# Where the expert scatter and the slot products stand in TensorE's row: tying them behind the next pair's up product

## The chip, the cores and the metric

The kernel runs on one core of a Trainium2 chip. The metric is the device time of one execution in microseconds (us): the median over the runs shown. Beside it stands one execution taken by the hardware profiler, whose trace gives the start and length of the instructions on TensorE (PE), its weight loads (PEld), VectorE (DVE), ScalarE (ACT), GpSimd (POOL) and the DMA queue of SyncE (SP).

## The reference

Two layers of a transformer trunk over 256 tokens of width 1024. Each layer is a token mixer (forgetting attention in layer 0, latent attention under a chunk mask in layer 1, "mixer B" below) and then a mixture of experts. 16 experts of width 512 stand in 4 groups; a router takes the best group of each token and two experts in it. Cut to the experts, for one layer:

```
h    = modulate(rmsnorm(x), shift, scale)
idx  = the two experts of each token, in its best group
g, u = h @ w_gate[e], h @ w_up[e]            # 1024 -> 512, for each expert e
y_e  = (silu(g) * u * routing_weight) @ w_down[e]   # 512 -> 1024
x    = x + gate * sum over a token's two experts of y_e
```

Everything is float32.

## The kernel before, in words

The experts are worked on in pairs, i = 0 to 7 in each layer, 64 token slots for each expert, so a pair fills 128 rows. `P[g]` are one-hot matrices of group g (two pairs) that say which token sits in which slot. The accumulators of the new x stay in four PSUM banks (0 to 3: two token halves by two column halves) for the whole expert stage. One pair goes like this:

- `wide("g", i, 4)` and `wide("u", i, 5)` (line 899): the gate product into bank 4 and the up product into bank 5, 16 matmuls each, two instructions in the trace for one matmul (float32). The weights come in pieces of at most 1 MB. After a product `done` gives the pieces' buffers back.
- silu on ScalarE (line 985), then `act`, the product of silu, up product and routing weight, on VectorE (line 996).
- four transposes of act into bank 4 (line 1003), copied to `aT` half by ScalarE, half by VectorE (lines 1006, 1007).
- the down product (line 1018) in two column halves, banks 6 and 7. Behind it VectorE multiplies by the layer's gate (`yb`, line 1031) and splits the result in two parts for a pass in a reduced float format (`yh`, lines 1033, 1034).
- `scatter(i)` (line 911): eight matmuls that add the pair's result into banks 0 to 3 by the transposed one-hot matrix `PT[i]`. It is written in pair i + 1, behind that pair's act. For the last pair it is written out behind each part of the down product (line 1044), followed by copies of x (line 1049, layer 0) or products with the final gain (`xg`, line 739, layer 1).
- `slots(i + 1, 5)` (line 883): two products that turn the one-hot matrix of the next pair, and VectorE's evictions of them (`PT`, and the routing weights `cs` that the next pair's act needs).
- after odd pairs, `fetch` (line 869): four times eight matmuls that gather the next group's tokens.

Before the up product of pair 4 (`OV`) stands a branch to an overflow path, which is not taken in the profiled execution (line 917).

All weights come over one DMA queue, on SyncE, in a fixed order through ten buffers of 1 MB (line 250) and some smaller tiles that are free in a stage (`Pieces`, line 262). A piece is issued when its buffer has been given back, so the queue waits for the product that read the buffer before.

The order of the instructions on each engine is set by a scheduler that works from the code's data dependences and its own estimate of times. It may put a scatter matmul anywhere behind its inputs: between down products, between gate products, or singly. `tc.issue_after(ins)` adds one rule: what is written inside stands behind the instruction `ins` on that engine. PSUM banks 4 and 5 serve in turn for gate, up, transposes, gathers and slot products.

Of the kernel before, what the change touches and what calls it, by code (L numbers as in the profile page):

```python
# [38 lines left out]
E = 16  # L39
# [4 lines left out]
OV = 4  # L44
# [29 lines left out]
def trunk_kernel(ctx, tc, A, out):  # L74
# [10 lines left out]
    def bank(i):  # L85
        return psp.tile([128, 512], F32, name=f"b{i}", tag=f"b{i}")
# [11 lines left out]
    def wide_rows(nm, l, i):  # L98
        return ((0, 4), (4, 2), (6, 2)) if l and nm == "u" and i == E // 2 - 1 else ((0, 4), (4, 4))
# [104 lines left out]
    u = A["kv_w_up"].rearrange("(p k) (a n) -> p k a n", k=2, a=2)  # L204
# [66 lines left out]
    def get(name):  # L271
        assert name in live, name
        return live[name]
# [11 lines left out]
    def done(name):  # L285
        assert stream[state["used"]][0] == name, (stream[state["used"]][0], name)
        drop()
        mods()
# [10 lines left out]
    def behind(i):  # L299
        return tc.issue_after(state["after"][i]) if state["after"][i] else ExitStack()  # L300
# [172 lines left out]
    def fin_bc(name, tag):  # L473
        rows = mod_rows(name)
        g_ = big.tile([128, D], F32, name=tag)
        ps = bank(MB)
        for h in range(2):
            if h:
                ps = bank(MB)
            for q in range(2):  # L480
                PE.matmul(ps[:, 256 * q:256 * q + 256], pick[:, 2 * h + q:2 * h + q + 1].to_broadcast([128, 128]), rows,
                          start=True, stop=True)
            SC.activation(g_[:, 512 * h:512 * h + 512], ps, AF.Copy)
        M[name] = g_
# [262 lines left out]
    def moe(l, G, sh, acc):  # L747
# [83 lines left out]
        def onehot(g):  # L831
            P[g] = wk.tile([128, T, 4, CAP], F32R, name="P", tag="zef", bufs=1)
            for t in range(T):
                at = V.tensor_tensor(P[g][:, t], iotas[:, None, :].to_broadcast([128, 4, CAP]),  # L834
                                     pos[:, t, 4 * g:4 * g + 4, None].to_broadcast([128, 4, CAP]), op=ALU.is_equal)
            return at.ins
# [43 lines left out]
        def slots(i, b):  # L880
            ps = bank(b).rearrange("p (t n) -> p t n", t=T)[:, :, 0:2 * E + 128]
            for t in range(T):
                PE.matmul(ps[:, t], P[i // 2][:, t, 2 * (i % 2):2 * (i % 2) + 2].rearrange("p e s -> p (e s)"), idc[:, t],
                          start=True, stop=True)
            PT[i] = wk.tile([128, T, 128], F32R, name="PT")
            V.tensor_copy(PT[i], ps[:, :, 2 * E:])
            for e in range(2):
                part = ps[64 * e:64 * e + 64, :, 0:2 * E].rearrange("p t (j e) -> p t j e", j=2)
                V.tensor_reduce(cs[64 * e:64 * e + 64, i:i + 1], part[:, :, :, 2 * i + e], axis=AX.XY, op=ALU.add)

        def wide(nm, i, b):
            ps = bank(b)
            for c, (k0, nk) in enumerate(wide_rows(nm, l, i)):
                ws = [get((nm, l, i, c, e)) for e in range(2)]
                for kk in range(nk):
                    k = k0 + kk
                    for e in range(2):
                        o = 128 * (i % 2) + 64 * e
                        last = PE.matmul(ps[64 * e:64 * e + 64, :], XG[i // 2, k // 4][:, k % 4, o:o + 64], ws[e][:, kk, :],  # L899
                                         start=k == 0, stop=k == 7).ins  # L900
                if i == 0 and nm == "g":
                    after[5] = last
                for e in range(2):
                    done((nm, l, i, c, e))
            return ps

        def scatter(i):
            for half in range(2):
                for t in range(T):
                    for j in range(2):  # L910
                        PE.matmul(acc[t, half], PT[i][:, t, :], yh[:, j, 512 * half:512 * half + 512],  # L911
                                  start=False, stop=False)
# [63 lines left out]
        for i in range(E // 2):  # L976
            pg = wide("g", i, 4)
            if i == OV:
                scatter(i - 1)
                overflow()  # L980
            if l and i == 0 and G2IN:
                with behind(5):
                    fin_bc("g2_1", "g2")
            sg = wk.tile([128, F], F32, name="sg", tag="t2", bufs=3)
            SC.activation(sg, pg, AF.Silu)  # L985
            if i == 0:
                slots(0, SL0)
                if l == 0:
                    with tc.issue_after(late):
                        rotary()  # L990
            turn_over = i % 2 and i < E // 2 - 1
            if turn_over:
                onehot(i // 2 + 1)
            pu = wide("u", i, 5)
            a = wk.tile([128, F], F32, name="act", tag="t2", bufs=3)
            V.scalar_tensor_tensor(a, sg, cs[:, i:i + 1], pu, op0=ALU.mult, op1=ALU.mult)  # L996
            if i and i != OV:
                scatter(i - 1)
            if l and i == 2:
                final_gain()  # L1000
            pa = bank(4)
            for k in range(4):
                PE.transpose(pa[:, 128 * k:128 * k + 128], a[:, k::4], ident)  # L1003
            aT = wk.tile([128, 4, 128], F32, name="aT", tag="t2", bufs=3)
            pav = pa.rearrange("p (a b) -> p a b", a=4)
            SC.activation(aT[:, 0:2], pav[:, 0:2], AF.Copy)  # L1006
            V.tensor_copy(aT[:, 2:4], pav[:, 2:4])
            if turn_over:
                for c in range(2):
                    fetch(i // 2 + 1, c, (5, 4)[c])  # L1010
            cols = down_cols(l, i)
            for p, (c0, n) in enumerate(cols):
                py = bank(6 + p % 2)
                cs_ = slice(c0, c0 + n)
                ws = [get(("d", l, i, p, e)) for e in range(2)]
                for k in range(4):
                    for e in range(2):
                        at = PE.matmul(py[64 * e:64 * e + 64, 0:n], aT[:, k, 64 * e:64 * e + 64], ws[e][:, k, :],  # L1018
                                       start=k == 0, stop=k == 3).ins
                if i == OV - 1 and p == 1:  # L1020
                    with tc.issue_after(at):
                        tc.mark_branch_hint_location(f"over{l}", "LikelyTaken", [mybir.EngineType.PE])
                for e in range(2):
                    done(("d", l, i, p, e))
                if p == 0 and turn_over:
                    for c in range(2, 4):
                        fetch(i // 2 + 1, c, (5, 4)[c % 2])
                if p == 0 and i < E // 2 - 1:
                    slots(i + 1, 5)
                yb = big.tile([128, 512], F32, name="yb", bufs=2)  # L1030
                V.tensor_tensor(yb[:, 0:n], py[:, 0:n], M[f"g2_{l}"][:, cs_], op=ALU.mult)  # L1031
                if len(cols) == 2 or p == 0:
                    SC.activation(yh[:, 0, cs_], yb, AF.Copy)  # L1033
                    V.tensor_tensor(yh[:, 1, cs_], yb, yh[:, 0, cs_].bitcast(F32), op=ALU.subtract)
                    parts_ = [(PT[i], yh[:, j, cs_]) for j in range(2)]
                else:
                    parts_ = [(PT[i].bitcast(F32), yb[:, 0:n])]
                if i == E // 2 - 1:
                    half, o = c0 // 512, c0 % 512
                    if l == 0 and p == 0:  # L1040
                        x.new()
                    for t in range(T):
                        for j, (pt, y_) in enumerate(parts_):
                            PE.matmul(acc[t, half][:, o:o + n], pt[:, t, :], y_, start=False,
                                      stop=o + n == 512 and j == len(parts_) - 1)
                        if o + n == 512:
                            ch = slice(512 * half, 512 * half + 512)
                            if l == 0:
                                V.tensor_copy(x[:, t, ch], acc[t, half])
                            squares(t, half, None, acc[t, half])  # L1050
                    if l and o + n == 512:
                        gains(half, acc)
# [69 lines left out]

    accs = attention(0, maskA, 1.0, proj_a, "wo0", "g1_0")
    moe(0, M["sc2_0"], M["sh2_0"], accs)


# [263 lines left out]
```

## Time and profile before

| | us |
|---|---|
| median of 3 runs | 857.45 (856.47 to 857.65) |
| profiled execution | 856.38 |
| its span in the trace | 854.3 |
| PE busy | 767.0 (90%) |
| DVE busy | 376.0 (44%) |
| ACT busy | 266.6 (31%) |
| POOL busy | 166.2 (19%) |

The mean granted TensorE clock was 0.97 of full speed. 294.30 MB were read from device memory, 346 GB/s over the span. The span begins with the first instruction of the trace and ends with the last; the profiled execution is 2.1 us longer, which lies around it. Busy shares are means over four stages: mixer A to about 207 us, experts of layer 0 to about 447, mixer B with the router to about 622, experts of layer 1 to the end.

### The profile page before, as it was taken

How to read it: one execution, taken by the hardware profiler on the slowest of the kernel's cores; microseconds unless marked ns; L12 is line 12 of the kernel's file. 1: busy time of each engine (PE TensorE's matmuls, PEld its weight loads, DVE VectorE, ACT ScalarE, POOL GpSimd, SP SyncE). 2: the span in 40 equal slices, each digit the busy share in tenths (PEclk: the TensorE clock that was granted, in tenths of full speed). 3: DMA queues.
4: the chain of work that ended last, by engine and by line, in shares of the span. 5: the costliest groups of instructions: out<-in, count | busy, mean ns of one | idle time of the engine just before them, and what ended most of it. 6: DMA issues, size and time to landing. Idle time of an engine off the chain costs nothing.

```text
span 854.3 us, 11932 instructions
## 1 busy us (share of the span) xinstructions
PE 767.0 (90%) x4522; PEld 441.9 (52%) x4522; DVE 376.0 (44%) x831; ACT 266.6 (31%) x578; POOL 166.2 (19%) x151
## 2 busy tenths in 40 slices
PE   4678999998999999899978798999799999999994
PEld 2477888765344343243327666777533534434332
DVE  2389599977112211221238949665712321122112
ACT  2346456534101011010127555765511110111002
POOL 1273567320000000000007755321100000000000
PEclk9699999999999999999998999999799999999998
DMA  9997897899999999999997769768789999999992
GB/s 347 383 376 272 275 347 261 315 380 392 414 397 394 417 402 403 418 407 403 414 397 270 231 226 362 293 222 273 269 292 402 402 374 413 367 393 398 402 392 82
DMA packets 102855, 296.32 MB, mean 347 GB/s; under 512 B 6992, under 2 KB 26624, under 8 KB 90496
## 3 DMA queue, kind: packets, MB, share of 16 engines
q1 hardware_dynamic: 101968, 293.79, 90.8%
q10 hardware_dynamic: 288, 1.05, 0.3%
q8 instruction: 39, 0.64, 0.3%
q0 software_dynamic: 528, 0.59, 0.2%
q14 instruction: 32, 0.26, 0.1%
HBM read 294.30 MB, written 1.05 MB: 346 GB/s over the span
## 4 chain that ended last, share of the span: by engine, by line
issue 28%; PE 23%; DVE 5%; DMA 2%; ACT 1%; POOLq 0%; POOL 0%; SPq 0%; another core or an unknown queue 0%; DVEq 0%; ACTq 0%
PE b L899 6%; PE b L1018 4%; PE b L522 2%; PE b L523 2%; PE b L524 2%; DVE macc L329 1%; DMA fg<-in_final_norm_g_dram 1%; PE b L911 1%; PE b L631 1%; DMA w<-in_w_mod_dram 1%; DVE wl L518 1%; DMA w<-in_exp_w_gate_dram 1%; PE b L321 1%; PE b L557 1%; PE b L593 1%
## 5 line engine op out<-in xcount | busy, mean ns | idle before, releaser
L899 PE MATMUL b<-w,XG 128*64 128x512 f32 x1024 | 239.0, 595 | 0.6 <-PEq L917 0.6
L518 POOL TENSOR_TENSOR wl<-w,wh 128x512 fp32r<-128x512 f32 (+3 forms) x90 | 132.4, 1487 | 354.0 <-ACT wh L517 350.5
L899 PEld LDWEIGHTS b<-w,XG 128*64 128x64 f32 x1024 | 78.2, 137 | 140.8 <-issue 135.3
L1018 PE MATMUL b<-w,aT 128*64 128x512 f32 (+1 forms) x528 | 125.8, 585 | 3.7 <-ACT aT L1006 3.7
L996 DVE SCALAR_TENSOR_TENSOR act<-sg,rcs,b 128x512 f32<-128x512 f32 x16 | 12.0, 747 | 211.3 <-PE b L899 211.3
L517 ACT ACTIVATE wh<-w 128x512 fp32r<-128x512 f32 (+3 forms) x136 | 76.6, 587 | 63.3 <-PE b L524 22.7
L1018 PEld LDWEIGHTS b<-w,aT 128*64 128x64 f32 x528 | 38.2, 136 | 66.0 <-issue 56.2
L329 DVE SCALAR_TENSOR_TENSOR macc<-w,cact,macc 128x1024 f32<-128x1024 f32 x42 | 63.6, 1513 | 1.2 <-DMA w<-in_w_mod_dram 0.7
L1033 ACT ACTIVATE yh<-yb 128x512 fp32r<-128x512 f32 x31 | 19.6, 631 | 113.2 <-DVE yb L1031 113.2
L518 DVE TENSOR_TENSOR wl<-w,wh 128x512 fp32r<-128x512 f32 (+2 forms) x46 | 44.3, 973 | 19.8 <-ACT wh L517 19.7
L1031 DVE TENSOR_TENSOR yb<-b,g 128x512 f32<-128x512 f32 (+1 forms) x33 | 22.2, 674 | 64.1 <-PE b L1018 64.1
L985 ACT ACTIVATE sg<-b 128x512 f32<-128x512 f32 x16 | 9.6, 598 | 119.9 <-PE b L899 119.9
L539 POOL TENSOR_TENSOR rs<-rs,mhalf 128x1 f32<-128x1 f32 (+1 forms) x9 | 5.4, 602 | 206.6 <-DVE rs L538 206.6
L321 PE MATMUL b<-w,cact 128*32 128x256 f32 x512 | 39.9, 418 | 6.0 <-DMA w<-in_w_mod_dram 5.7
L524 PE MATMUL b<-h,wl 128*128 128x256 f32 (+1 forms) x136 | 40.5, 299 | 4.7 <-DVE wl L518 4.3
L522 PE MATMUL b<-h,wh 128*128 128x256 f32 (+1 forms) x136 | 40.3, 300 | 3.5 <-ACT h L579 3.5
L1006 ACT ACTIVATE aT<-b 128x256 f32<-128x256 f32 x16 | 6.1, 384 | 117.1 <-PE b L1003 117.1
L869 PEld LDWEIGHTS b<-P,xs 128*128 128x128 f32 x256 | 34.4, 203 | 15.2 <-DVE XG L875 6.5
L869 PE MATMUL b<-P,xs 128*128 128x256 f32 x256 | 39.3, 304 | 1.6 <-DVE P L834 1.6
L523 PE MATMUL b<-h,wh 128*128 128x256 f32 (+1 forms) x136 | 39.5, 292 | 0.0
L911 PE MATMUL b<-yh,PT 128*128 128x512 f32 x112 | 34.4, 422 | 2.1 <-ACT yh L1033 2.1
L523 PE MATMUL b<-wl,h 128*128 128x256 f32 (+1 forms) x96 | 30.0, 316 | 2.9 <-POOL wl L518 2.4
(296 smaller groups left out, 1208.8 us busy)
## 6 DMA issues: line engine op xcount, KB each, us to landing
w<-in_exp_w_down_dram SPq DMA_DIRECT2D x50, 1024.0 KB, 12.5
w<-in_w_mod_dram SPq DMA_DIRECT2D x48, 1024.0 KB, 8.9
w<-in_exp_w_gate_dram SPq DMA_DIRECT2D x48, 1024.0 KB, 12.8
w<-in_exp_w_up_dram SPq DMA_DIRECT2D x48, 1024.0 KB, 13.0
w<-in_a_w_in_dram SPq DMA_DIRECT2D x12, 1024.0 KB, 12.4
w<-in_exp_w_gate_dram SPq DMA_DIRECT2D x42, 256.0 KB, 7.2
w<-in_exp_w_up_dram SPq DMA_DIRECT2D x40, 256.0 KB, 5.9
w<-in_kv_w_mod_dram SPq DMA_DIRECT2D x8, 1024.0 KB, 7.0
```

The lines of the kernel that those rows point to most:

```text
L321: PE.matmul(acc[32 * q:32 * q + 32, :], cact[:, k:k + 1].to_broadcast([128, 32]), w[:, kk, 256 * q:256 * q + 256], start=k == 0, stop=k == 7)
L329: V.scalar_tensor_tensor(acc, w[:, kk, :], cact[:, k:k + 1], acc, op0=ALU.mult, op1=ALU.add)
L517: SC.activation(hi, src, AF.Copy)
L518: lo_eng.tensor_tensor(lo, src, hi.bitcast(F32), op=ALU.subtract)
L522: PE.matmul(ps, l[0], r_[0], start=start, stop=False)
L523: PE.matmul(ps, l[0], r_[1], start=False, stop=False)
L524: PE.matmul(ps, l[1], r_[0], start=False, stop=stop)
L869: at = PE.matmul(ps[:, 256 * kk:256 * kk + 256], xs[n % 2, n // 2][:, 128 * k:128 * k + 128], P[g][:, n // 2].rearrange("p e s -> p (e s)" ...
L899: last = PE.matmul(ps[64 * e:64 * e + 64, :], XG[i // 2, k // 4][:, k % 4, o:o + 64], ws[e][:, kk, :], start=k == 0, stop=k == 7).ins
L911: PE.matmul(acc[t, half], PT[i][:, t, :], yh[:, j, 512 * half:512 * half + 512], start=False, stop=False)
L1018: at = PE.matmul(py[64 * e:64 * e + 64, 0:n], aT[:, k, 64 * e:64 * e + 64], ws[e][:, k, :], start=k == 0, stop=k == 3).ins
L1031: V.tensor_tensor(yb[:, 0:n], py[:, 0:n], M[f"g2_{l}"][:, cs_], op=ALU.mult)
```

## The change

In each pair, what stands in the code behind act now gets a rule: it is to stand behind the last matmul of that pair's up product on TensorE. In pairs 1 to 3 and 5 to 7 that is the scatter of the pair before. In pairs 0 and 4 there is none (the scatter of pair 3 stays ahead of the overflow branch, without a rule), and the slot products for the next pair are put there, in bank 7 in place of bank 5 and no longer behind the first half of the down product.

```
                 if i == 0 and nm == "g":
                     after[5] = last
+                ends[nm] = last
...
+        ends = {}
...
             a = wk.tile([128, F], F32, name="act", tag="t2", bufs=3)
             V.scalar_tensor_tensor(a, sg, cs[:, i:i + 1], pu, op0=ALU.mult, op1=ALU.mult)
-            if i and i != OV:
-                scatter(i - 1)
+            with tc.issue_after(ends["u"]):
+                if i in (0, OV):
+                    slots(i + 1, 7)
+                else:
+                    scatter(i - 1)
...
-                if p == 0 and i < E // 2 - 1:
+                if p == 0 and i < E // 2 - 1 and i not in (0, OV):
                     slots(i + 1, 5)
```

The changed kernel has six lines more, so its scatter is line 914, its transposes 1009, its down products 1024 and the last pair's scatter 1050. The first place is TensorE's row from pair 4 of layer 0 to the transposes of pair 5. Before (b_5958 is the second half of pair 4's down product, b_5975 and b_6005 are gate and up of pair 5, b_1736 to b_1739 the accumulators):

```order
L911 MATMUL b_1736<-yh,PT 128x512
L911 MATMUL b_1738<-yh,PT 128x512
L1018 MATMUL b_5958<-w,aT 64x512 x7
L899 MATMUL b_5975<-w,XG 64x512
L911 MATMUL b_1737<-yh,PT 128x512
L911 MATMUL b_1739<-yh,PT 128x512
L899 MATMUL b_5975<-w,XG 64x512 x15
L899 MATMUL b_6005<-w,XG 64x512 x16
L1003 MATMUL b_6040<-idc,act 128x128 x4
```

The same stretch of the changed kernel:

```order
L1024 MATMUL b_5958<-w,aT 64x512 x8
L899 MATMUL b_5975<-w,XG 64x512 x16
L899 MATMUL b_6005<-w,XG 64x512 x16
L914 MATMUL b_1736<-yh,PT 128x512 x2
L914 MATMUL b_1738<-yh,PT 128x512 x2
L914 MATMUL b_1737<-yh,PT 128x512 x2
L914 MATMUL b_1739<-yh,PT 128x512 x2
L1009 MATMUL b_6040<-idc,act 128x128 x4
```

The scatter of pair 4 stood in three pieces in and behind its own down product and inside the gate product of pair 5; now it is one run between the up product and the transposes. In both layers the transposes of pairs 1 to 3 and 5 to 7 now have such a run ahead of them, and those of pairs 0 and 4 have the two slot products. Before, a run stood there in three places: pair 1 of layer 0, and pairs 1 and 3 of layer 1.

The second place is VectorE's row at the end of layer 0's experts, from the first half's yh (b_6316 and b_6346 are the two halves of pair 7's down product; the wl are weight splits for mixer B). Before:

```order
L1034 TENSOR_TENSOR yh<-yb,yh 128x512
L1049 COPY x<-b_1736 128x512
L1049 COPY x<-b_1738 128x512
L518 TENSOR_TENSOR wl<-w,wh 128x288 x2
L1031 TENSOR_TENSOR yb<-b_6346,g_2389 128x512
```

The same stretch of the changed kernel:

```order
L1040 TENSOR_TENSOR yh<-yb,yh 128x512
L518 TENSOR_TENSOR wl<-w,wh 128x288
L1055 COPY x<-b_1736 128x512
L518 TENSOR_TENSOR wl<-w,wh 128x288
L1055 COPY x<-b_1738 128x512
L518 TENSOR_TENSOR wl<-w,wh 128x288
L1037 TENSOR_TENSOR yb<-b_6346,g_2389 128x512
```

One weight split has moved ahead of the yb of the second half. On TensorE the last two of the four scatter matmuls that these copies wait for now stand two matmuls before the end of the down product; before, all four stood behind its first matmul of that half.

The third place is TensorE's row at the end of layer 1 (b_12263 is the first half of pair 7's down product, b_12288 and b_12301 are two quarters, b_7767 to b_7770 the accumulators). Before:

```order
L1003 MATMUL b_12255<-idc,act 128x128 x4
L1018 MATMUL b_12263<-w,aT 64x512 x8
L1018 MATMUL b_12288<-w,aT 64x256 x8
L1018 MATMUL b_12301<-w,aT 64x256 x8
L1044 MATMUL b_7767<-yh,PT 128x512
L1044 MATMUL b_7769<-yh,PT 128x512
```

The same stretch of the changed kernel:

```order
L914 MATMUL b_7770<-yh,PT 128x512 x2
L1009 MATMUL b_12255<-idc,act 128x128 x4
L1024 MATMUL b_12263<-w,aT 64x512 x8
L1024 MATMUL b_12288<-w,aT 64x256 x8
L1024 MATMUL b_12301<-w,aT 64x256
L1050 MATMUL b_7767<-yh,PT 128x512
L1050 MATMUL b_7769<-yh,PT 128x512
L1050 MATMUL b_7767<-yh,PT 128x512
L1050 MATMUL b_7769<-yh,PT 128x512
L1024 MATMUL b_12301<-w,aT 64x256 x7
```

The scatter of pair 6 now stands ahead of the transposes, and the first half's own scatter stands behind one matmul of the last quarter in place of all eight. At the start of layer 1's experts, five modulation matmuls stood ahead of the first gate product on TensorE; one does now, and the other four stand inside and behind that product. In mixer B, where no line has changed, the scheduler has put many instructions of all engines in another order.

## Rows read from the trace of the kernel before

**Rows 1.** The page: GB/s moved, in 40 equal slices of the span.

```profile
GB/s 347 383 376 272 275 347 261 315 380 392 414 397 394 417 402 403 418 407 403 414 397 270 231 226 362 293 222 273 269 292 402 402 374 413 367 393 398 402 392 82
```

**Rows 2.** Stretches: from:to, length, busy us (count) by engine, clock, DMA share, GB/s.

```profile
215.00:440.00 225.00, 213.03 (x999) 85.36 (x996) 43.11 (x87) 26.13 (x46) 0.55 (x1) 1.00 1.03 407
625.00:836.00 211.00, 204.21 (x950) 83.75 (x948) 42.20 (x87) 24.11 (x44) 0.61 (x1) 1.00 1.01 386
...
350.00:360.00 10.00, 7.93 (x32) 2.67 (x32) 2.50 (x4) 1.26 (x2) 0.00 (x0) 1.00 1.01 422
...
470.00:480.00 10.00, 7.46 (x44) 6.10 (x43) 9.91 (x17) 4.68 (x8) 9.21 (x9) 1.00 0.45 140
...
610.00:620.00 10.00, 6.71 (x44) 5.80 (x43) 5.36 (x27) 1.69 (x3) 0.00 (x0) 0.54 0.58 222
```

**Rows 3.** Waits of the DMA queue, whole span: us in total, times, longest.

```profile
SPq L250 <- PE b L899: 111.8, 49, 8.1
```

**Rows 4.** Waits of TensorE from 200 us on: us in total, times, longest.

```profile
PE b L1003 <- DVE act L996: 11.1, 12, 0.9
```

**Rows 5.** Timeline of TensorE, layer 0, pair 4: start, length, instruction, idle before.

```profile
344.72 0.75 PE L1003 MATMUL b<-idc,act 128*128 128x128 f32 x4 [0.92 <-DVE act L996]
...
357.62 1.46 PE L911 MATMUL b<-yh,PT 128*128 128x512 f32 x4 [1.44 <-ACT yh L1033]
...
373.87 0.75 PE L1003 MATMUL b<-idc,act 128*128 128x128 f32 x4 [0.91 <-DVE act L996]
```

**Rows 6.** Timeline of TensorE, layer 1, pair 2 to pair 3.

```profile
693.47 0.75 PE L1003 MATMUL b<-idc,act 128*128 128x128 f32 x4 [0.93 <-DVE act L996]
...
715.55 2.14 PE L911 MATMUL b<-yh,PT 128*128 128x512 f32 x8
717.53 0.63 PE L1003 MATMUL b<-idc,act 128*128 128x128 f32 x4
```

**Rows 7.** DMA queue, last up pieces of layer 0: issues, then time to landing.

```profile
L250 SPq DMA_DIRECT2D w<-in_exp_w_up_dram x2: 328/356/385, 411.7 to 412.2; - x2
...
DMA to landing us min/median/max: 12.7/13.7/14.8
```

**Rows 8.** Timeline of TensorE, end of layer 0: last up matmuls, transposes of pair 7.

```profile
428.25 4.03 PE L899 MATMUL b<-w,XG 128*64 128x512 f32 x16
...
433.19 0.75 PE L1003 MATMUL b<-idc,act 128*128 128x128 f32 x4 [0.91 <-DVE act L996]
```

**Rows 9.** Timeline of TensorE, end of layer 1.

```profile
829.30 2.31 PE L899 MATMUL b<-w,XG 128*64 128x512 f32 x8
...
832.51 0.75 PE L1003 MATMUL b<-idc,act 128*128 128x128 f32 x4 [0.91 <-DVE act L996]
...
843.68 2.06 PE L1044 MATMUL b<-yb,PT 128*128 128x256 f32 x8 [1.65 <-DVE yb L1031]
```

**Rows 10.** Timeline of VectorE, end of layer 0.

```profile
440.93 1.29 DVE L1049 COPY x<-b 128x512 f32<-128x512 f32 x2 [0.59 <-PE b L1044]
```

**Rows 11.** The page's groups: instruction, count, busy, mean ns, idle before.

```profile
L329 DVE SCALAR_TENSOR_TENSOR macc<-w,cact,macc 128x1024 f32<-128x1024 f32 x42 | 63.6, 1513 | 1.2 <-DMA w<-in_w_mod_dram 0.7
```

**Rows 12.** Timeline of the DMA queue, start of layer 1's experts.

```profile
620.22 5.99 SPq L250 DMA_DIRECT2D w<-in_exp_w_up_dram  x2
```

**Rows 13.** Timeline of TensorE, ahead of layer 1's first gate product.

```profile
621.23 1.05 PE L321 MATMUL b<-w,cact 128*32 128x256 f32 x10
```

**Rows 14.** DMA queue, last up pieces of layer 1: issues, then time to landing.

```profile
L250 SPq DMA_DIRECT2D w<-in_exp_w_up_dram x2: 328/356/383, 814.5 to 814.9; - x2
...
DMA to landing us min/median/max: 9.3/9.8/10.2
```

**Rows 15.** DMA queue, last down pieces of layer 1: issues, then time to landing.

```profile
L250 SPq DMA_DIRECT2D w<-in_exp_w_down_dram x2: 540/540/540, 827.4 to 828.2; - x2
...
DMA to landing us min/median/max: 7.6/7.9/8.1
```

**Rows 16.** Timeline of VectorE, end of layer 1.

```profile
842.60 0.69 DVE L739 TENSOR_TENSOR xg<-b,fg 128x512 f32<-128x512 f32 x1 [2.97 <-ACT junk L532]
```

## The prediction

> **What bounds the kernel now.** I read the page's slices first. Its row of bytes moved shows two long runs of slices with some 400 GB/s, the ninth to the 21st (171 to 448 us) and the 31st to the 39th (641 to 833) [rows 1]. Those are the two expert stages. The view by stretches says the same in numbers: 1.03 and 1.01 of the engines' time, 407 and 386 GB/s, with TensorE busy for 213 of 225 us and 204 of 211 us [rows 2]. So two things are nearly full at once, and which of them sets a stage's end has to be worked out. A pair of experts reads three matrices of 2 MiB for each of two experts, 12.58 MB; at 407 GB/s that is 30.9 us. The DMA queue's own waits say that it stands mostly behind products that still hold its buffers [rows 3]. The queue is therefore held back by TensorE in its issues, but the engines under it never run dry: earlier issues make a longer line and not more bytes in a microsecond.
>
> TensorE's own largest wait is the one that the change aims at: the transposes wait for act 12 times, 11.1 us in all, 0.9 us each [rows 4].
>
> **What each pair gains on TensorE.** In pair 4 of layer 0 the transposes start at 344.72, those of pair 5 at 373.87 [rows 5]: 29.15 us. Inside are the wait for act (0.91 at its end), a wait of 1.44 for yh because the second half of the scatter stands straight behind the down product, and lone products between scatter pieces. The form that the change gives to pairs exists before, whole, in one place, from pair 2's transposes in layer 1 to pair 3's: down, gate, up, the eight scatter products in one run, and then the transposes without a wait, 693.47 to 717.53 = 24.06 us; the run of eight costs 1.98 (715.55 to 717.53) [rows 6]. So pair 4 can save 29.15 - 24.06 = 5.1. Worked in the same way from the starts of the other transposes, layer 0 could save about 16 us (pairs 2 and 6: 2.4 each, pair 3: 2, pair 5: 3.5, the first wait 0.9) and layer 1, where less was scattered, about 9. In pairs 0 and 4 two slot products (0.43) cover part of the wait of 0.91; what is left, 0.5 twice a layer, is inside these numbers. No arithmetic is added, and no transfer.
>
> **What the weights let through in layer 0.** A pair in the new form takes 24.06 us, its weights 30.9. TensorE can only use the lead that the weights still have. The last pieces of layer 0's up product are issued at 411.7 to 412.2 and land at most 14.8 us later, so the last at 426.9 [rows 7]. The up product's last 16 matmul rows begin at 428.25, and the second expert's first is two rows in, at 428.68 [rows 8] (a row is 0.215: 16 of them take 4.03, eight take 2.31 [rows 9]). The lead is 1.77 us. That is all that the end of the up product can gain, of the 16. Behind it now stands the scatter: the transposes of pair 7 come at 433.19 [rows 8] - 1.77 - 0.91 (the wait for act, now covered) + 1.97 = 432.5, a gain of 0.7. Then the order of layer 0's end changes: VectorE now has two copies of x (1.29 for the two [rows 10]) and two weight splits between the last scatter product into their banks and the second half's yb, where before they ran while the down product was still at work. As the bank that x copies is finished two matmuls (four rows, 0.86) before the down product's end, I put the delay at 1.1, with 0 and 1.7 as bounds. Layer 0 as a whole: 0.7 - 1.1 = **0.4 lost**.
>
> **The mixer between.** The scheduler orders mixer B anew as well, on all engines; no line of the diff is in it. VectorE is busy for 9.91 of 10 us at 470 to 480, so one of the modulation steps of 1.51 us [rows 2, 11] that is put ahead of work that TensorE needs, or behind it, moves the end by about its length. I find moves in both directions and no reason for a sign: **0, bounds 2.5 either way**.
>
> **What the weights let through in layer 1.** The weight stream of this layer restarts behind releases of TensorE (between its first two issues, 5.99 us from 620.22 on [rows 12]), and the gate product now starts behind two of ten modulation rows (1.05 us from 621.23 [rows 13]). So the whole stream comes about **0.8 earlier** (bounds 0 and 0.9). The last up pieces are issued at 814.9 and land 10.2 later at the latest, at 825.1 [rows 14]; their use is two rows behind 829.30, at 829.73 [rows 9]. The lead is 4.6, and with the earlier stream the up product can end 5.4 earlier. TensorE offers 9, so the weights decide again. As in layer 0 the scatter (1.97) takes the place of the wait (0.91): the transposes come at 832.51 - 5.4 + 1.06 = 828.2. The down pieces do not hold this up: the last are issued at 828.2 and land within 8.1 [rows 15], at 836.3 and with the earlier stream at 835.5, and their use moves behind four scatter products, to about 836.5.
>
> At the end TensorE now issues the four scatter products of the first half after one matmul of the last quarter, not after all of them. Before, yb of a quarter stood on VectorE behind xg, which came 2.97 us after the work before it, when those scatter products had been read once [rows 16], and TensorE then idled 1.65 for a yb [rows 9]. I follow the new order with the durations of the same rows and get the last scatter run about **1.0 earlier** (bounds 0 and 1.7).
>
> **Sum.** + 0.4 (layer 0) + 0 (mixer) - 0.8 (restart) - 4.6 (lead of the up product) + 1.06 (scatter for wait) - 1.0 (end) = -4.9 on the profiled execution's 856.38, so 851.5. The median of the three runs lies 1.07 above that execution: **852.5 us**.
>
> **Rivals.** *The transfers go faster when the queue is further ahead.* Slices of layer 0 reach 414 to 418 GB/s [rows 1] against a mean of 407. At 418 a pair takes 0.8 us less; over the three pairs of each layer in which TensorE would wait this is 5 us more, 847.5. If transfers did not bind at all, both savings would come in full, 16 + 9 = 25, about 832; the share of 1.03 speaks against it. The Trainium skill (Perfetto Trace Analysis, Roofline) gives a single core about 435 GB/s over its 16 DMA engines; by it, as an estimate, a pair's weights would take 28.9 us, and three waiting pairs in each layer would give 12 us more, 840.5. No slice of this trace holds that pace.
>
> *No change.* The lead in layer 1 is real only if the stream keeps its times. If the restart gives nothing (0.8 back), the end gains nothing (1.0 back) and mixer B's new order takes its 2.5, the time is 852.5 + 4.3 = 856.8.
>
> *Slower: the clock.* In the new form TensorE is busy for 24.06 of 30.9 us of a pair, 78%, and waits for weights in between. The granted clock fell where it did less: 0.54 over 610 to 620, with 6.71 of 10 us busy; it stayed at 1.00 with 7.93 of 10 busy at 350 to 360 [rows 2]. 0.54 is all but half of full speed, 1.2 of 2.4 GHz. A stretch like 610 to 620 costs 4.6 us (0.46 of 10). In the middle of a layer this is hidden, since TensorE waits for weights anyway; in the last pair of each layer nothing hides it. It has to happen at both ends to decide the sign: 852.5 + 9.2 = 861.7; at one end alone the time is 857, no change. The Trainium skill's rule (TensorE: Matmul & The Clock Gate, HAM oscillation) speaks for this rival: a matmul loop that waits for a transfer in each tile has its clock cut again and again. The row at 350 to 360 does not follow it, but its waits were for other engines and shorter.
>
> **How the numbers follow.** The forecast, weights bind in both layers with the bounds above, has 0.62. Faster transfers, from some us to the full saving, have 0.14, of which 0.06 below 847.5. No change has 0.15 and slower by the clock, or by a mixer order beyond its bound, 0.09. A measurement of this kernel tells about 0.2%, 1.7 us, from no change. The forecast and the faster transfers are faster by more than that, 0.76 with nothing from the others; the no-change case is nearly all within it. The range goes from 847.5, transfers at the best slices' pace, to 857.0, where the no-change case ends with all its bounds against me; about 0.06 lies below and 0.13 above.
>
> **What would show it.** In the changed profile the row of waits for act should fall from 12 to about four short ones, and eight scatter products in one run should stand before most transposes. In layer 0 waits of TensorE for landings should appear at gate and up products from the middle of the stage on, some 14 us in sum, and the transposes of pair 7 should stand near 432.5: this is the step on which most hangs. In layer 1 the transposes of pair 7 should stand near 828, apart from what the mixer shifts, and the last landing near 835.5. I am wrong if the DMA share falls below 1 in layer 0 with transposes well before 432, if the stage of layer 1 starts more than 2.5 us off, or if the granted clock falls at the end of a layer.

## The result: 11 us faster, outside the predicted range

The changed kernel takes 846.46 us in the median (845.37 to 850.70, 4 runs), the kernel before 857.55 beside it (4 runs). The ratio is 0.9867, 95% interval 0.9846 to 0.9887, so 1.1 to 1.5% faster. A second measurement on another occasion gives 847.01 against 858.18, ratio 0.9884 (0.9854 to 0.9913). The profiled execution took 845.37, its span 843.3; before it was 854.3, so 11.0 of span are to be found, where 4.9 had been forecast.

The stretches of the changed kernel, with the columns of [rows 2]; the last two lie in mixer B:

```profile
215.00:440.00 225.00, 208.61 (x1002) 89.69 (x1000) 43.57 (x88) 26.79 (x48) 0.55 (x1) 1.00 1.03 405
625.00:836.00 211.00, 205.76 (x990) 91.27 (x986) 46.49 (x95) 27.14 (x53) 0.61 (x1) 1.00 1.00 384
525.00:535.00 10.00, 8.25 (x58) 6.53 (x58) 10.00 (x21) 5.69 (x16) 4.43 (x4) 1.00 1.03 399
535.00:545.00 10.00, 9.63 (x75) 7.78 (x74) 8.64 (x40) 8.41 (x27) 2.22 (x3) 1.00 1.02 407
```

Layer 0's stretch has the same DMA share and 405 in place of 407 GB/s, and TensorE is less busy in it: 208.6 in place of 213.0 us. It now waits for weights, as its waits from 200 us on show (us in total, times, longest):

```profile
PE b L899 <- DMA w<-in_exp_w_up_dram: 6.9, 7, 1.4
...
PE b L899 <- DMA w<-in_exp_w_gate_dram: 4.5, 4, 1.3
...
PE b L1050 <- ACT yh L1039: 2.8, 2, 2.1
...
PE b L1009 <- DVE act L999: 1.6, 3, 0.5
```

The wait for act, 12 times and 11.1 us before [rows 4], is three short ones, in pairs 0 and 4, which have only slot products there. In its place stand eleven waits for landings, 11.4 us, of which TensorE in the kernel before has none. All but one, 0.6 us, lie in layer 0.

The end of layer 0 on TensorE, which answers to [rows 8]:

```profile
430.62 2.13 PE L914 MATMUL b<-yh,PT 128*128 128x512 f32 x8
432.59 0.63 PE L1009 MATMUL b<-idc,act 128*128 128x128 f32 x4
...
446.20 1.46 PE L1050 MATMUL b<-yh,PT 128*128 128x512 f32 x4 [2.14 <-ACT yh L1039]
450.80 1.54 PE L557 MATMUL b<-idc,xn 128*128 128x128 f32 x6 [3.14 <-DVE xn L545]
```

Pair 7's transposes start 0.60 earlier than before, behind a run of eight scatter products, and mixer B's first product (line 557) starts at 450.80, where before it started at 450.75. VectorE in between, which answers to [rows 10], shows where the 0.60 went:

```profile
442.86 0.69 DVE L1055 COPY x<-b 128x512 f32<-128x512 f32 x1 [2.61 <-PE b L1050]
443.47 0.45 DVE L518 TENSOR_TENSOR wl<-w,wh 128x288 fp32r<-128x288 f32 x1
443.84 0.68 DVE L1055 COPY x<-b 128x512 f32<-128x512 f32 x1
444.44 0.45 DVE L518 TENSOR_TENSOR wl<-w,wh 128x288 fp32r<-128x288 f32 x1
444.80 0.68 DVE L1037 TENSOR_TENSOR yb<-b,g 128x512 f32<-128x512 f32 x1
```

The copies start 1.93 later than before, the second half's yb stands behind them, and TensorE waits 2.14 for it. So layer 0 with its end comes out even, 16 us of saving on TensorE and all.

The end of layer 1 on TensorE, which answers to [rows 9], and the last up pieces, which answer to [rows 14] (issues, then time to landing):

```profile
820.82 2.13 PE L914 MATMUL b<-yh,PT 128*128 128x512 f32 x8
822.80 0.63 PE L1009 MATMUL b<-idc,act 128*128 128x128 f32 x4
...
829.70 1.29 PE L1050 MATMUL b<-yh,PT 128*128 128x512 f32 x4
...
832.79 1.99 PE L1050 MATMUL b<-yb,PT 128*128 128x256 f32 x8
```

```profile
L250 SPq DMA_DIRECT2D w<-in_exp_w_up_dram x2: 328/355/382, 805.5 to 805.9; - x2
...
DMA to landing us min/median/max: 12.1/12.5/13.0
```

Mixer B, from its first product of line 557 to its last score products, before and then with the change:

```profile
450.75 1.54 PE L557 MATMUL b<-idc,xn 128*128 128x128 f32 x6 [3.14 <-DVE xn L545]
...
582.26 0.38 PE L592 MATMUL b<-ka,qa 96*128 96x128 f32 x2
```

```profile
450.80 1.54 PE L557 MATMUL b<-idc,xn 128*128 128x128 f32 x6 [3.14 <-DVE xn L545]
...
578.86 0.39 PE L592 MATMUL b<-ka,qa 96*128 96x128 f32 x2
```

The transposes of pair 7 start 9.72 earlier. Mixer B ended 3.40 earlier, the last up piece lands 6.22 earlier (805.92 + 12.98 = 818.90, against 825.12), and TensorE follows it more closely. The last scatter run starts at 832.79 without a wait, 10.89 earlier than in [rows 9].

### The profile page after: what moved, and what is told of

It is laid out like the page before. It is cut to its first block, busy times and chain, and to the rows that moved or that the text cites. A ratio compares the mean times of both kernels' runs of the same rounds, so it can differ in the third digit from the quotient of the medians.

```text
span 843.3 us, 11931 instructions
## 1 busy us (share of the span) xinstructions
PE 757.0 (90%) x4522; PEld 449.9 (53%) x4522; DVE 375.4 (45%) x831; ACT 266.0 (32%) x578; POOL 165.3 (20%) x151
## 4 chain that ended last, share of the span: by engine, by line
PE 23%; issue 22%; DMA 7%; DVE 5%; ACT 3%; POOLq 0%; POOL 0%; another core or an unknown queue 0%; SPq 0%; ACTq 0%; DVEq 0%
PE b L899 5%; DMA w<-in_exp_w_up_dram 5%; PE b L1024 3%; PE b L522 2%; PE b L523 2%; PE b L524 2%; DVE macc L329 2%; DMA w<-in_exp_w_down_dram 2%; PE b L869 1%; PE b L321 1%; DVE wl L518 1%; DMA fg<-in_final_norm_g_dram 1%; PE b L631 1%; PE b L593 1%; PE b L592 1%
## 5 line engine op out<-in xcount | busy, mean ns | idle before, releaser
L899 PE MATMUL b<-w,XG 128*64 128x512 f32 x1024 | 234.5, 595 | 13.6 <-DMA w<-in_exp_w_up_dram 6.9
L899 PEld LDWEIGHTS b<-w,XG 128*64 128x64 f32 x1024 | 81.6, 137 | 153.2 <-issue 124.8
L1024 PE MATMUL b<-w,aT 128*64 128x512 f32 (+1 forms) x528 | 121.9, 586 | 4.0 <-ACT aT L1012 4.0
L329 DVE SCALAR_TENSOR_TENSOR macc<-w,cact,macc 128x1024 f32<-128x1024 f32 x42 | 68.9, 1640 | 1.1 <-DMA w<-in_w_mod_dram 0.7
L875 DVE TENSOR_SCALAR XG<-b,c_sc,c_sh 128x256 f32<-128x256 f32 x32 | 17.4, 543 | 32.8 <-ACT XG L877 32.5
## 6 DMA issues: line engine op xcount, KB each, us to landing
w<-in_exp_w_gate_dram SPq DMA_DIRECT2D x42, 256.0 KB, 7.2
w<-in_exp_w_up_dram SPq DMA_DIRECT2D x40, 256.0 KB, 6.3
```

What stands on the lines that cost most here:

```text
L329: V.scalar_tensor_tensor(acc, w[:, kk, :], cact[:, k:k + 1], acc, op0=ALU.mult, op1=ALU.add)
```

## The experiments

Every kernel was run beside the kernel before. The first question was why mixer B, in which no line changed, became shorter. Its order turned out to hang on the end of layer 0: in all kernels below that load all bytes, except `l0_tail_order`, the order of mixer B's instructions on TensorE and VectorE is the changed kernel's where the scatter in pair 7 of layer 0 has the rule, and that of before where it has not. (In the records of l0_pair7 and scatter_only, two products of line 631 that run side by side start in the other order.)

**The rule in pair 7 of layer 0 alone** (`l0_pair7`):

```
+            if l == 0 and i == 7:
+                with tc.issue_after(ends["u"]):
+                    scatter(i - 1)
+            elif i and i != OV:
                 scatter(i - 1)
```

> The rule stands in one place alone: pair 7 of layer 0; everything else is written as before, and mixer B comes out of the scheduler in the changed kernel's order, word for word. Theory (mixer B's 3.4 us come from its order alone): nothing makes the weights or TensorE earlier in layer 0, so pair 7's transposes come 1.06 later (scatter 1.97 for the wait of 0.91), at 434.25, the first transposes of mixer B about 1.7 later, at 452.4, mixer B itself is 3.4 shorter, and layer 1 is as before: 1.7 less than the kernel before, 855.8. Rival (mixer B gained because layer 0's weights and products had been handed on earlier): no gain in the mixer, 1.7 more than before, 859.2.

Measured: 857.48 against 858.11, ratio 0.9987 (0.9966 to 1.0008). The rival's 1.002 lies outside the interval, but the profile does not bear out the theory as it stood either: mixer B took 131.7 us, as before, though in the new order. Its clock was at half from 498.4 to 501.8 and from 532.5 to 539.3 (0.78 over 535 to 545). And layer 1 was not "as before": written as before, it came out of the scheduler with the scatters of its pairs 5 and 6 in more pieces and that of pair 4 in other places, and its stage took 195.2 in place of 192.3 us.

**The rule in layer 1 alone** (`layer1_only`):

```
+            if l == 1:
                 with tc.issue_after(ends["u"]):
                     if i in (0, OV):
                         slots(i + 1, 7)
                     else:
                         scatter(i - 1)
+            elif i and i != OV:
+                scatter(i - 1)
```

> The rule, for scatter and slot products, in layer 1 alone; mixer B stands in the order of before. Theory (layer 1's stage gives the rest, 11.0 - 3.4 = 7.6, of which about 3 because the weight stream itself gets shorter when TensorE gives buffers back earlier): 7.6 less than before, 849.9, with layer 1's last up piece landing 2.5 to 3 earlier than before's 825.1, near 822.3. Rival (the stream's extra 3 us came from mixer B, by other pieces being under way when layer 1 starts): 4.6 less, 852.9, last up piece at 825.

Measured: 850.17 against 858.11, ratio 0.9916 (0.9895 to 0.9937), 5.4 to 9.0 us. The rival's 4.6 lies outside. The last up piece landed at 822.26. So layer 1 gains at least the 5.3 that were forecast for it, and mixer B (131.5) has no part in that. The theory's reason, a stream that gets shorter, fell with the profiles below; that its 822.3 was met was luck.

**The slot products alone** (`slots_only`):

```
-            with tc.issue_after(ends["u"]):
-                if i in (0, OV):
-                    slots(i + 1, 7)
-                else:
-                    scatter(i - 1)
+            if i in (0, OV):
+                with tc.issue_after(ends["u"]):
+                    slots(i + 1, 7)
+            else:
+                scatter(i - 1)
```

> The slot products are tied and put in bank 7 in pairs 0 and 4 of both layers; the scatter has no rule, as before. Mixer B in the order of before. Theory (the scatter carries the change): two waits for act a layer fall by 0.4 and layer 0 is held by its weights, so 0 to 1.5 less than before, 857. Rival (the slot products carry it, since the next pair's act and gathers wait for their eviction): 4 or more less.

Measured: 857.54 against 858.11, ratio 0.9985 (0.9969 to 1.0002). The scatter carries the change.

**The scatter alone** (`scatter_only`):

```
             with tc.issue_after(ends["u"]):
-                if i in (0, OV):
-                    slots(i + 1, 7)
-                else:
+                if i and i != OV:
                     scatter(i - 1)
...
-                if p == 0 and i < E // 2 - 1 and i not in (0, OV):
+                if p == 0 and i < E // 2 - 1:
                     slots(i + 1, 5)
```

> The rule for the scatter alone; the slot products stay in bank 5 behind the first half of the down product. Mixer B in the changed kernel's order. Theory (the slot products count for 0.5 a layer at most, and layer 0 is held by weights): as the changed kernel, 846.5 to 847.5, 10 to 11 less than before.

Measured: 845.35 against 857.97, ratio 0.9848 (0.9827 to 0.9868). This is the change, as far as can be measured. Its profiled execution took 853.13; what was longer in it is read below.

**The rule everywhere but in pair 7 of layer 0** (`all_but_l0_pair7`; the condition is `(l, i) != (0, 7)`):

> The changed kernel without the rule in one place, pair 7 of layer 0, where the scatter comes out behind the down product and inside the gate product as before. Mixer B comes out in the order of before, word for word. Theory: layer 0's weights end where they did (last up piece at 427.0), the scatter is no longer behind them, and the wait for act is back: pair 7's transposes at 431.5 and not 432.6, mixer B's first transposes at 449.1 and not 450.8; mixer B takes 131.6 from there to its last score product and not 128.0; layer 1 as with the change. In sum 3.6 - 1.7 = 1.9 more than the changed kernel, 848.7. Rival (mixer B's time has nothing to do with the order): 1.7 less than the changed kernel, 845.

Measured: 848.70 against 857.97, ratio 0.9888 (0.9865 to 0.9910). The end of layer 0 in its profile:

```profile
431.81 0.74 PE L1012 MATMUL b<-idc,act 128*128 128x128 f32 x4 [0.91 <-DVE act L999]
...
449.37 1.97 PE L557 MATMUL b<-idc,xn 128*128 128x128 f32 x8 [3.15 <-DVE xn L545]
```

The wait for act is back, and the transposes are still 0.78 earlier than with the change, in the presence of the same weights: a scatter behind the last weights costs more than the wait it covers. Mixer B took 132.9. The median is the theory's to 0.1, but that it is above the changed kernel's is clear only from the profile, since the intervals of the two medians overlap.

**The rule in layer 0 alone** (`layer0_only`; the condition is `l == 0`):

> The rule for scatter and slot products in layer 0 alone, mixer B in the changed kernel's order, layer 1 as before. Theory: pair 7's transposes in layer 0 at 432.6, as with the change, of the 16 us that TensorE saves nothing is left at the end of the stage; the mixer gives 3.4 where its clock holds, so 853.5 to 855, 3 to 4 less than before. Rival (layer 0 hands its saving on): 846 or less.

Measured: 856.89 against 857.97, ratio 0.9990 (0.9971 to 1.0009), less than expected. The transposes of pair 7 in layer 0 came at 433.18, in an execution that began the stage 2.3 later than the changed kernel's, and mixer B took 128.2, both as the theory has it. But layer 1 gave the mixer's gain back: there the scatter of pair 4, without a rule, stood inside the gate product, and that of pair 5 came out in four pieces, of which three stand here:

```profile
788.87 0.73 PE L914 MATMUL b<-yh,PT 128*128 128x512 f32 x2
789.43 0.35 PE L883 MATMUL b<-idc,P 128*128 128x160 f32 x2
789.71 1.07 PE L899 MATMUL b<-w,XG 128*64 128x512 f32 x2
790.71 0.73 PE L914 MATMUL b<-yh,PT 128*128 128x512 f32 x2
791.37 3.65 PE L899 MATMUL b<-w,XG 128*64 128x512 f32 x14
794.95 0.73 PE L914 MATMUL b<-yh,PT 128*128 128x512 f32 x2
```

Pair 5 took 32.91 from transposes to transposes, 2.0 more than before (30.87). Layer 0's 16 us are not handed on: the rival's 846 is far off.

**Layer 0 with half its gate and up bytes** (`light_before`, `light_after`), one execution each; only the first half of the columns is loaded and used twice, so the number of products is the same:

```
-                    nc.sync.dma_start(v, src)
+                    h_ = 256 if name[0] in ("g", "u") and name[1] == 0 else src.shape[2]
+                    nc.sync.dma_start(v[:, :, 0:h_], src[:, :, 0:h_])
...
-    ws[e][:, kk, :],
+    ws[e][:, kk, 0:256].unsqueeze(1).to_broadcast([128, 2, 256]) if l == 0 else ws[e][:, kk, :],
```

> The kernel before with half the bytes of layer 0's gate and up weights: only the first 256 columns of each are loaded and used twice, with the same matmuls; so its output is not the reference's. A pair's weights then take about 20.6 us of transfers in place of 30.9, and TensorE is the bound of layer 0. Expected from the transposes of pair 0 to those of pair 7 in layer 0: about the 201.4 of before, within 3, since TensorE hardly waited for weights there.

> The changed kernel with the same half loads of layer 0's gate and up weights. Theory (in layer 0 the change's saving on TensorE is real and only the weights take it back): from pair 0's transposes to pair 7's 13 to 17 less than in the kernel before with half loads, no waits for landings, and pair 7's transposes near 418. Rival (the saving of 16 was worked out wrongly, other waits come in its place): less than 5.

Measured, from the transposes of pair 0 to those of pair 7: 185.15 and 184.24. The first expectation failed: with the lighter loads the scheduler itself put four of layer 0's scatters, whole, ahead of the transposes (4 waits for act from 208 to 430 us, 3.7 us), so the pair does not tell the two orders apart. The other half of the question is answered. With the rule and half the bytes no wait for a landing is left, and the transposes of pair 7 stand 15.5 earlier than in the changed kernel:

```profile
415.07 2.14 PE L920 MATMUL b<-yh,PT 128*128 128x512 f32 x8
417.05 0.63 PE L1015 MATMUL b<-idc,act 128*128 128x128 f32 x4
```

TensorE's own time for the stage in this order is 184.2; with all bytes it is 200.5. The weights hold 16.3 us of it. It is 17.2 less than the 201.4 of the kernel before, so the saving of about 16 that the prediction worked out for TensorE is there.

**Half of layer 1's last run behind the gate product** (`l1_pair7_split` and, beside the changed kernel `changed_again`, `l1_split_again`):

```
+            elif l and i == E // 2 - 1:
+                with tc.issue_after(ends["g"]):
+                    scatter(i - 1, (0,))
+                with tc.issue_after(ends["u"]):
+                    scatter(i - 1, (1,))
```

> The changed kernel, but in pair 7 of layer 1 half of the scatter is tied behind the gate product, half behind the up product. Mixer B in the changed kernel's order. Theory (at the end of a layer TensorE waits for the last weights, so a scatter ahead of the last pieces is free and one behind them costs its 1.97 less the 0.91 that it covers): the half of 1.0 goes into the wait of 1.2 ahead of the second up piece, and the end comes 1.0 earlier than with the change, 845.4; the transposes of pair 7 still do not wait for act. Rival (the last up piece is not what holds the up product's end): no difference from the change, 846.5.

> The changed kernel as it is, timed beside the next one on the same chip. Theory: 11 less than before, ratio 0.987.

> The changed kernel with half of layer 1's last scatter run behind the gate product, once more, beside the changed kernel. Theory (what was 3 slower in the first run's profile was the weight stream, which varies by some us from execution to execution; the last weights hold the end): equal to the changed kernel or up to 1.0 better. Rival (a scatter run inside gate and up makes the end worse): 2 to 3 slower than the changed kernel in the median.

Measured: first 849.66 (ratio 0.9900, 0.9865 to 0.9936), then 848.35 beside 847.01 of the changed kernel (0.9893, 0.9870 to 0.9916, beside 0.9884). These intervals show no difference. The profile of the first shows why the 1.0 is there and is worth nothing:

```profile
816.54 1.20 PE L914 MATMUL b<-yh,PT 128*128 128x512 f32 x4
...
826.00 0.69 PE L1015 MATMUL b<-idc,act 128*128 128x128 f32 x4
827.22 1.07 PE L1030 MATMUL b<-w,aT 128*64 128x512 f32 x2 [0.53 <-ACT aT L1018]
828.51 1.94 PE L1030 MATMUL b<-w,aT 128*64 128x512 f32 x8 [0.21 <-DMA w<-in_exp_w_down_dram]
```

The transposes start 2.96 after the last up piece has landed (823.04), and not 3.90. Behind them the down product now waits for its own pieces, and the last scatter run comes as long after the last up landing as in the changed kernel (15.5, table below).

**The copies of x behind the second half's yh** (`l0_tail_order`; `lo` is the instruction that writes that yh):

```
+                            with tc.issue_after(lo):
                                 V.tensor_copy(x[:, t, ch], acc[t, half])
```

> The changed kernel, but the copies of x at the end of layer 0 are tied behind the second half's yh, so that they do not stand ahead of its yb. The scheduler puts mixer B back nearly into the order of before. Theory: the wait of 2.14 of TensorE for yh falls to 1.4 and mixer B's first transposes come 0.7 to 0.9 earlier, near 450.0, but the mixer takes up to 3.5 more; 2 to 3 slower than the changed kernel, 849. Rival (the time is set at the end of layer 0, not by the mixer's order): 0.8 less than the changed kernel.

Measured: 850.89 against 857.97, ratio 0.9912 (0.9888 to 0.9936). The wait for yh fell from 2.14 to 1.54, but the four copies then stand in a row (2.47) ahead of the normalisation, and mixer B begins 18.2 after the transposes of pair 7, as with the change. No gain there; mixer B, back nearly in the old order, took 131.4. The rival's 0.8 less than the changed kernel would be a ratio of 0.986 to 0.988, outside the interval.

**Six numbers from the profile of each kernel.** Mixer B: from the first product of line 557 there to the start of the last score product (line 592). Clock: the granted clock over 525 to 545. Stage: layer 1's transposes of pair 0 to those of pair 7. T7: the transposes of pair 7 after the landing of the last up piece. End: the start of the last scatter matmul after that landing. Stream: from the landing of the piece that the kernel before issues at 626.33 to the last up landing.

| kernel | mixer B | clock | stage | T7 | end | stream |
|---|---|---|---|---|---|---|
| before | 131.6 | 0.91 | 192.3 | 7.39 | 20.2 | 191.7 |
| slots_only | 132.7 | 0.83 | 191.2 | 9.57 | 22.4 | 187.2 |
| l0_pair7 | 131.7 | 0.83 | 195.2 | 9.74 | 21.4 | 193.2 |
| layer0_only | 128.2 | 1.00 | 195.2 | 11.00 | 22.6 | 192.0 |
| changed | 128.2 | 1.00 | 184.9 | 3.90 | 15.5 | 188.9 |
| changed_again | 127.9 | 1.00 | 187.4 | 3.91 | 15.5 | 191.4 |
| layer1_only | 131.5 | 0.91 | 185.4 | 3.89 | 15.5 | 188.5 |
| scatter_only | 131.0 | 0.91 | 189.2 | 3.89 | 15.5 | 193.0 |
| all_but_l0_pair7 | 132.9 | 0.83 | 187.9 | 3.90 | 15.5 | 189.3 |
| l0_tail_order | 131.4 | 0.91 | 188.7 | 3.90 | 15.5 | 192.8 |
| l1_pair7_split | 127.9 | 1.00 | 187.8 | 2.96 | 15.5 | 192.7 |
| l1_split_again | 127.9 | 1.00 | 183.8 | 2.98 | 15.5 | 188.9 |

## Why the prediction was wrong, point by point

**Layer 0 was right.** Transposes of pair 7 were forecast at 432.5 and came at 432.59; the lead of 1.77 was all that the weights let through; the waits for landings were forecast at some 14 us and are 10.8 in the stage. The end was forecast 0.4 later and is 0.05 later. The rival of faster transfers is out: from a piece that landed at 181.8 before to the stage's last down piece (437.8) the stream takes 256.0 before, 256.0 with the change, and 255.4 to 256.5 in the other ten kernels with all bytes, however far ahead the issues are: the stage's last up piece is issued at 406.75 with the change and at 412.16 before, and lands at 427.00 and 426.91. The Trainium skill's 435 GB/s over 16 DMA engines (Perfetto Trace Analysis, Roofline) is not reached in this stage: 405 with the change.

**The exchange of the wait for the scatter, and the end of layer 1, were right.** From the last up landing to the transposes it was 7.39 and is 3.90; forecast was 7.39 - 4.61 + 1.06 = 3.84. It is 3.9 in all six profiles that have layer 1's rule whole. From the transposes to the last scatter matmul it was 12.85 and is 11.60, 1.25 less; forecast was 1.0. This 1.25 goes with the order at the end of layer 1 and not with the rule there: l0_pair7 and layer0_only, without the rule in layer 1, have it too (End less T7 is 11.6 in both, 12.85 before and in slots_only). One sentence in that step was too sure: the down pieces were said not to hold this up. With the change they just do not; the split run shows that they stand right behind.

**The step that failed first: "The mixer between ... 0, bounds 2.5 either way".** It is -3.4, in a term whose bound was set too tight. Mixer B's order is a by-product of what stands at the end of layer 0: where one scatter stands, and, in l0_tail_order, the copies of x. In the old order it took 131.5 to 132.9 in four profiles, in the new order 127.9 to 128.2 in five and 131.0 and 131.7 in two. These two are the ones whose clock fell near 535, and near 500 as well; the old order fell near 535 in all four. The means are 132.2 and 129.0. The stretches of scatter_only and of the kernel before, with the columns of [rows 2], scatter_only first:

```profile
525.00:535.00 10.00, 8.27 (x57) 6.88 (x55) 9.24 (x20) 6.28 (x20) 4.11 (x4) 0.97 1.02 394
535.00:545.00 10.00, 9.35 (x62) 6.94 (x62) 7.45 (x30) 6.62 (x19) 2.72 (x3) 0.86 1.02 417
```

```profile
525.00:535.00 10.00, 7.05 (x44) 4.99 (x42) 9.31 (x22) 5.95 (x18) 4.54 (x4) 0.95 1.03 403
535.00:545.00 10.00, 8.83 (x63) 7.31 (x63) 6.12 (x34) 6.92 (x20) 1.70 (x2) 0.88 1.02 407
```

From the first product of line 617 there, 76 to 78 us into the mixer, to its last score product it is 54.2 before, 53.2 in scatter_only with a like fall, 51.9 with the change and the full clock. So of the 3.4 some 1.3 is the clock near 535, and the other 2.1 comes with the order. The part ahead of line 617 (77.4 before, 76.3 with the change) is not the same work in both, since 446 instructions of TensorE stand in it before and 434 with the change; so the 2.1 can't be split by parts. In it are TensorE's waits between 500 and 560 for attention rows from the other engines. Before:

```profile
PE b L617 <- DVE yatt L611: 2.2, 1, 2.2
PE b L631 <- ACT pT L622: 1.8, 2, 1.2
```

and with the change:

```profile
PE b L617 <- DVE yatt L611: 1.6, 1, 1.6
PE b L631 <- ACT pT L622: 0.2, 1, 0.2
```

These waits fall by 2.2, while those ahead of line 617 grow from 6.8 to 7.6, because more time goes to waits for weight splits there; where the rest of the 2.1 comes from is not shown. The share of the clock rests on two executions of the new order with a fall; the old order was never seen without one, so what it would take at full clock is not shown.

**The step that failed second: the lead in layer 1 taken from one execution.** "Weights decide again" was right, but the sum fixed their times to those of the kernel before, less 0.8. The restart gave almost nothing: that stream's start moved 3.5, all but 0.1 of it mixer B's. With that the prediction's own sign of being wrong came, a start of layer 1's stage more than 2.5 off (its first transposes moved 2.4). The stream itself took 188.9 against 191.7, which gave 2.7 more. At first I took this for an effect of the change (buffers given back earlier), and the expectations of layer1_only say so. The table contradicts it: the stream takes 187.2 to 193.2 in kernels without layer 1's rule and 188.5 to 193.0 in kernels with it. It varies from execution to execution: by 3.8 between the two of the split kernel, by 6.0 over all twelve kernels. Without the rule the stage takes 191.2 to 195.2 whatever the stream does, so TensorE holds it, and a short stream only makes a longer lead; with the rule it follows the stream, 184.9 to 189.2 in six profiles, mean 187.3. So with the change layer 1's end waits for the weights in each of these six. Against before and slots_only, whose mean is 191.8, that is 4.5, and 1.25 at the end: 5.75, against 5.3 in the forecast. What the two profiled executions show beyond it is the luck of a short stream.

**The sum.** For the two profiled executions: layer 0 +0.05, mixer B -3.4, restart -0.1, stream -2.7, lead and scatter -3.5, end -1.25, in sum -10.9 of 11.0. Of the shortfall of 6.1 mixer B has 3.4 and the stream, with the restart, 2.0. Over the executions profiled it is less than in these two: 3.2 for mixer B (132.2 less 129.0), 4.5 and 1.25 for layer 1, in sum 9.0, below the first interval measured for the change (9.7 to 13.2) and inside the second (7.5 to 12.5). What lies between the mixer's end and layer 1's first transposes is not in this sum; it took 57.8 before and 58.9 and 57.8 in the two profiles of the changed kernel. Layer 1 alone gained 5.4 to 9.0 against 5.7 from this. Some 2 of the 11 that the medians show are thus not accounted for, and their cause stays open.

**The rivals.** Slower by the clock did not come: TensorE waited ten times for landings in layer 0 and its granted clock was 1.00 over the whole stretch. The rival's share of 78% was that of a pair without gathers; over the stretch TensorE was busy for 208.6 of 225 us. The Trainium skill's rule on loops that wait for a transfer in each tile (TensorE: Matmul & The Clock Gate, HAM oscillation) did not show at waits of at most 1.4 us. No change did not come either, since the mixer's term went the other way.

## What to carry to other kernels

Where a scheduler sets the order, a rule in one place can reorder a stage in which no line changed; compare the order of every stage, and give a reordered stage a bound with room for its waits and for a fall of the clock in it. A lead read from one execution is a sample: where a stage changes from being held by an engine to being held by the transfers, its end takes over their spread. An engine's saving in a stage that is held by transfers is worth its lead and no more, which can be read before the change from the landings of the last pieces.

## What the runs showed of the hardware

The weight stream of layer 0 repeats to within 1.1 us in 256 over twelve kernels, that of layer 1 spreads over 6.0 in 190; the extra time comes in single pieces. One up piece, for example, landed 2.28 after the piece before it in l1_pair7_split, where with the change it took 0.69, and another 3.98 after in l0_tail_order, where with the change it took 2.48. What delays them is not shown. The granted clock fell to half (0.50, the lower of its two levels, 1.2 GHz) at other places of mixer B in executions of the same order: in the new order from about 466 to 470 in six of seven, in scatter_only from 500.2 to 503.6 and from 534.3 to 537.7 as well, in l0_pair7 from 498.4 to 501.8 and from 532.5 to 539.3. In the new order a fall of 3.4 us near 535 goes with 1.3 us of the mixer's time from line 617 on (53.2 in scatter_only against 51.9), one of 6.8 with 2.6 (54.5 in l0_pair7), in one execution each.
